# Batch normalisation, one core: loads and stores without pacing waits

## The chip, the cores and the metric

The kernel runs on one core of a Trainium2 chip. The metric is the device time of one execution in microseconds (us), the median of several runs. Lower is better. The chip's profiler also recorded one execution; all views of the profile come from that one.

## The reference

The input is 32 images of 256 channels of 128 x 128 float32 values. Each channel is scaled and shifted by stored statistics:

```
mean, var, gamma, beta: one value per channel (256)
out = gamma * (x - mean) / sqrt(var + 1e-5) + beta      # x, out: (32, 256, 128, 128) float32
```

So every element is read once, multiplied by `scale = gamma / sqrt(var + eps)` of its channel, has `shift = beta - mean * scale` added, and is written once: 537 MB in and 537 MB out.

## The kernel before

A tile is half the channels of one image: 128 channels on the 128 partitions, with the 16384 pixels of each as one row of 64 KB. A tile has 8.4 MB, and there are `NT` = 64 of them (`order` lists them: the first 128 channels of all images, then the others). Three buffers `t0`, `t1`, `t2` (`NBUF` = 3) take them in turn; tile i lies in buffer i mod 3 and is computed in place.

Nothing is scheduled by a tool; each engine works down its own list, and semaphores hold it.

- **SyncE** issues the loads (queue q1 of the profile). Tile 0 comes in two halves (lines 87 and 94) with the four small vectors of statistics between them (line 90), then tiles 1 and 2 (line 96). From tile 3 on there are two waits for each load: on `stored` (line 102), which counts that the store of tile i-3 has left the buffer, and on `vdone` (lines 103 and 104), which counts VectorE's pieces: the load of tile i goes out when VectorE has done the first piece of tile i-1.
- **VectorE** computes `scale` and `shift` once (lines 106 to 124), then the left part of each tile with `tensor_scalar` (line 129). A tile has a first piece of `STEP` = 2560 columns, which waits for the tile's landing, and a second up to column `VCOLS` = 14336. In the last tile the second ends at `VLAST` = 9216. Tile 0 has two pieces of its own, one for each half that lands.
- **ScalarE** computes the rest of each tile with `activation` (line 140), 2048 columns, and 7168 in the last tile. Before the last tile it waits for both of VectorE's pieces (line 161) and for the store of tile i-1 to have landed (lines 163 and 164). Then it issues the store of the whole tile (line 153, queue q10), which waits for `adone`, its own computation. So there is one store at a time. In the last tile ScalarE starts when the tile lands, beside VectorE, and the store waits for both.

So at most one load and one store are under way at a time after the first three loads, and ScalarE, though it computes last, runs only once a store has landed. At the end SyncE waits for the last stores (line 171) and clears the semaphores. One transfer moves 128 rows of 64 KB over 16 DMA engines, 8 rows on each.

Of the kernel before, what the change touches and what calls it, by code (L numbers as in the profile page):

```python
# [8 lines left out]
NBUF = 3  # L9
PAD = 936  # L10


STEP = 2560
VCOLS = 14336
VLAST = 9216

# [2 lines left out]
def kernel(  # L19
# [9 lines left out]
    nc = tc.nc  # L29
# [8 lines left out]
    NT = N * NCB  # L38
# [5 lines left out]
    xr = x.rearrange("n (cb p) h w -> (n cb) p (h w)", p=P)  # L44
    outr = out.rearrange("n (cb p) h w -> (n cb) p (h w)", p=P)

    def tile_of(name, *shape):
        return nc.alloc_sbuf_tensor(name, list(shape), f32)
# [11 lines left out]
    bufs = [tile_of(f"t{s}", P, HW) for s in range(NBUF)]  # L60
# [4 lines left out]
    loaded = [sems[f"loaded{s}"] for s in range(NBUF)]  # L65
    stored = [sems[f"stored{s}"] for s in range(NBUF)]
    early, vdone, adone, fetched, vec, act = (sems[n] for n in names[2 * NBUF :])
# [5 lines left out]
    def step(inst, sem=None, value=None):  # L73
        if sem is not None:
            inst._wait_ge(sem, value)
        elif count[0]:
            inst._wait_ge(vec, count[0])
        inst.then_inc(vec, 1)
        count[0] += 1
        return count[0]  # L80

    left, right = slice(0, HW // 2), slice(HW // 2, HW)
    last = NT - 1
    order = [n * NCB + cb for cb in range(NCB) for n in range(N)]

    with tc.tile_critical():  # L86
        nc.sync.dma_start(out=bufs[0][:, left], in_=xr[order[0]][:, left]).then_inc(early, 16)
        zeroed = step(nc.vector.memset(rows[:], 0.0))  # L88
        for r, ap in enumerate((running_var, gamma, beta, running_mean)):
            inst = nc.sync.dma_start(out=rows[0:NE, r * C : (r + 1) * C], in_=ap.partition_broadcast(NE))  # L90
# [8 lines left out]

    for i in range(NBUF, NT):  # L100
        s, turn = i % NBUF, i // NBUF
        nc.sync.wait_ge(stored[s], 16 * turn)
        inst = nc.sync.dma_start(out=bufs[s][:], in_=xr[order[i]]).then_inc(loaded[s], 16)
        inst._wait_ge(vdone, 2 * (i - 1) + 1)

    step(nc.vector.memset(eps_t[:], eps))  # L106
    step(nc.vector.transpose(out=turned[:], in_=rows[:]), fetched, 16 * NPAR)  # L107
# [3 lines left out]
    for q in range(NQ):  # L111
# [3 lines left out]
        out=std_t[:],  # L115
        in_=var_t,
# [7 lines left out]
    ready = step(nc.vector.tensor_sub(out=shift_t[:], in0=beta_t, in1=ms_t[:]))  # L124
    nc.vector.wait_ge(vec, ready)

    def vector_part(i, first, end):
        t, cb = bufs[i % NBUF], order[i] % NCB
        return nc.vector.tensor_scalar(  # L129
            out=t[:, first:end],  # L130
            in0=t[:, first:end],
            scalar1=scale_t[:, cb : cb + 1],
            scalar2=shift_t[:, cb : cb + 1],
            op0=mybir.AluOpType.mult,
            op1=mybir.AluOpType.add,
        ).then_inc(vdone, 1)

    def scalar_part(i, first):
        t, cb = bufs[i % NBUF], order[i] % NCB
        return nc.scalar.activation(  # L140
            out=t[:, first:],
            in_=t[:, first:],
            func=mybir.ActivationFunctionType.Identity,
            bias=shift_t[:, cb : cb + 1],
            scale=scale_t[:, cb : cb + 1],
        ).then_inc(adone, 1)

    def landed(i):
        return loaded[i % NBUF], 16 * (i // NBUF + 1)

    def store(i):
        s = i % NBUF
        nc.scalar.dma_start(out=outr[order[i]], in_=bufs[s][:])._wait_ge(adone, i + 1).then_inc(stored[s], 16)
# [1 line left out]
    vector_part(0, 0, HW // 2)._wait_ge(early, 16)  # L155
    vector_part(0, HW // 2, VCOLS)._wait_ge(*landed(0))
    for i in range(1, NT):
        vector_part(i, 0, STEP)._wait_ge(*landed(i))
        vector_part(i, STEP, VLAST if i == last else VCOLS)
    for i in range(last):  # L160
        nc.scalar.wait_ge(vdone, 2 * (i + 1))
        inst = scalar_part(i, VCOLS)
        if i:
            inst._wait_ge(stored[(i - 1) % NBUF], 16 * ((i - 1) // NBUF + 1))
        store(i)
    scalar_part(last, VLAST)._wait_ge(*landed(last))
    nc.scalar.wait_ge(vdone, 2 * NT)
    store(last)

    for s in range(NBUF):  # L170
        nc.sync.wait_ge(stored[s], 16 * ((NT - s + NBUF - 1) // NBUF))
# [31 lines left out]
```

## Time and profile before

| | |
|---|---|
| median of 3 runs | 2481.28 us (2480.5 to 2481.8) |
| the profiled execution: its own time | 2480.81 us |
| its span in the profile | 2479.5 us |
| VectorE (DVE) busy | 508.7 us (21%) |
| ScalarE (ACT) busy | 139.8 us (6%) |
| moved by the DMA engines | 1073.85 MB, 433 GB/s over the span |
| a load, issue to landing | 37.0 us (median) |
| a store, issue to landing | 36.5 us (median) |

The span runs from the first to the last instruction that the profiler recorded; the execution's own time has 1.31 us more around it. Busy times count computing instructions only: an engine that waits for a semaphore or issues a transfer is not busy. "Issue to landing" is the time from the issuing instruction until the transfer's semaphore is full, and so has in it the time in which the transfer stands in its queue or shares the DMA engines with another. In the lists of waits and instructions, a name with a q behind it (SPq, ACTq) is the engine's sequencer, which issues transfers.

### The profile page before, as it was taken

What the parts mean: (1) busy time and instruction counts of PE and PEld (TensorE: products, weight loads), DVE (VectorE), ACT (ScalarE), POOL (GpSimd) and SP (SyncE); (2) the same over time, 40 slices, a digit from 0 to 9 for tenths busy, and PEclk for the clock granted to TensorE, in tenths of its full rate; (3) what the DMA queues carried; (4) which work ended last, traced back from release to release, by engine and by line L of the source; (5) the groups of instructions that cost most, each with busy time, mean ns of one, the idle gap of its engine ahead of it and who ended that gap; (6) DMA issues with size and microseconds to landing.
All of it is one profiled execution on the core that took longest, in us unless ns stands there. A gap on an engine that the chain in (4) does not pass through costs nothing.

```text
span 2479.5 us, 514 instructions
## 1 busy us (share of the span) xinstructions
DVE 508.7 (21%) x139; ACT 139.8 (6%) x66; POOL 0.2 (0%) x4
## 2 busy tenths in 40 slices
DVE  2122121221212212122121221212212122121220
ACT  0000000000000000000000000000000000000001
POOL 0000000000000000000000000000000000000000
DMA  9999999999999999999999999999999999999999
GB/s 412 435 438 427 437 438 429 436 438 429 435 438 430 435 439 430 433 438 433 431 438 432 432 438 432 432 438 432 432 438 433 431 438 433 431 438 435 430 438 410
DMA packets 18708, 1073.85 MB, mean 433 GB/s; under 512 B 2128, under 2 KB 2192, under 8 KB 2192
## 3 DMA queue, kind: packets, MB, share of 16 engines
q1 hardware_dynamic: 9488, 536.94, 50.1%
q10 hardware_dynamic: 9216, 536.88, 50.0%
q14 instruction: 4, 0.03, 0.0%
HBM read 536.94 MB, written 536.87 MB: 433 GB/s over the span
## 4 chain that ended last, share of the span: by engine, by line
DMA 92%; DVE 4%; another core or an unknown queue 2%; ACT 0%; issue 0%; SPq 0%; DVEq 0%
DMA t<-in_x_dram 92%; DVE t L129 4%; ACT t L140 0%; SPq L90 0%; DVE rows L88 0%; DVEq L98 0%; SPq L86 0%
## 5 line engine op out<-in xcount | busy, mean ns | idle before, releaser
L129 DVE TENSOR_SCALAR t<-t,scale_t,shift_t 128x11776 f32<-128x11776 f32 (+2 forms) x128 | 505.2, 3989 | 1928.4 <-DMA t<-in_x_dram 1928.3
L140 ACT ACTIVATE t<-t,shift_t,scale_t 128x2048 f32<-128x2048 f32 x64 | 138.2, 2159 | 2297.3 <-DMA out_dram<-t 2274.5
L107 DVE STREAM_TRANSPOSE turned<-rows 32x1024 f32<-32x1024 f32 x1 | 1.2, 1232 | 7.6 <-DMA rows<-in_running_mean_dram 7.6
L114 ACT ACT_TABLE_LOAD x1 | 1.3, 1283 | 6.4 <-PEq L98 6.4
L88 DVE MEMSET rows<- 32x1024 f32 x1 | 0.9, 912 | 1.2 <-SPq L86 1.2
L106 DVE MEMSET eps_t<- 128x1 f32 x1 | 0.1, 59 | 4.4 <-PEq L98 4.4
L114 ACT ACTIVATE std_t<-par,eps_t 128x2 f32<-128x2 f32 x1 | 0.3, 295 | 8.5 <-DVE par L112 8.5
L112 DVE COPY par<-turned 32x8 f32<-32x8 f32 x4 | 0.7, 162 | 0.1
L121 DVE RECIPROCAL rstd_t<-std_t 128x2 f32<-128x2 f32 x1 | 0.2, 165 | 0.4 <-ACT std_t L114 0.4
L122 DVE TENSOR_TENSOR scale_t<-par,rstd_t 128x2 f32<-128x2 f32 x1 | 0.2, 161 | 0.0
L123 DVE TENSOR_TENSOR ms_t<-par,scale_t 128x2 f32<-128x2 f32 x1 | 0.2, 161 | 0.0
L124 DVE TENSOR_TENSOR shift_t<-par,ms_t 128x2 f32<-128x2 f32 x1 | 0.2, 160 | 0.0
L187 POOL MEMSET const-bfloat16-1.0<- 128x1 bf16 x1 | 0.1, 101 | 0.0
L187 POOL MEMSET const-uint8-127<- 128x1 uint8 x1 | 0.1, 101 | 0.0
L187 POOL MEMSET const-float32-0.0<- 128x1 f32 x1 | 0.1, 98 | 0.2 <-issue 0.2
L187 POOL MEMSET const-float32-1.0<- 128x1 f32 x1 | 0.1, 98 | 0.0
## 6 DMA issues: line engine op xcount, KB each, us to landing
t<-in_x_dram SPq DMA_DIRECT2D x2, 4096.0 KB, 16.0
out_dram<-t ACTq DMA_DIRECT2D x64, 36.5
t<-in_x_dram SPq DMA_DIRECT2D x63, 37.0
rows<-in_running_var_dram SPq DMA_DIRECT2D x1, 16.0 KB, 11.2
rows<-in_gamma_dram SPq DMA_DIRECT2D x1, 16.0 KB, 11.0
rows<-in_beta_dram SPq DMA_DIRECT2D x1, 16.0 KB, 10.7
rows<-in_running_mean_dram SPq DMA_DIRECT2D x1, 16.0 KB, 10.7
```

The costliest lines, as they stand in the source:

```text
L88: zeroed = step(nc.vector.memset(rows[:], 0.0))
L106: step(nc.vector.memset(eps_t[:], eps))
L107: step(nc.vector.transpose(out=turned[:], in_=rows[:]), fetched, 16 * NPAR)
L112: placed = step(nc.vector.tensor_copy(out=flat[q * B : (q + 1) * B], in_=blocks[:, :, q, 0]))
L114: nc.scalar.activation(out=std_t[:], in_=var_t, func=mybir.ActivationFunctionType.Sqrt, bias=eps_t[:], scale=1.0,)._wait_ge(vec, placed).t ...
L121: step(nc.vector.reciprocal(out=rstd_t[:], in_=std_t[:]), act, 1)
L122: step(nc.vector.tensor_mul(out=scale_t[:], in0=gamma_t, in1=rstd_t[:]))
L123: step(nc.vector.tensor_mul(out=ms_t[:], in0=mean_t, in1=scale_t[:]))
L124: ready = step(nc.vector.tensor_sub(out=shift_t[:], in0=beta_t, in1=ms_t[:]))
L129: return nc.vector.tensor_scalar(out=t[:, first:end], in0=t[:, first:end], scalar1=scale_t[:, cb : cb + 1], scalar2=shift_t[:, cb : cb + 1 ...
L140: return nc.scalar.activation(out=t[:, first:], in_=t[:, first:], func=mybir.ActivationFunctionType.Identity, bias=shift_t[:, cb : cb + 1] ...
L187: nc = _bacc.Bacc("TRN2", target_bir_lowering=False, num_devices=1)
```

## The change

The waits that hold transfers back for another reason than their data are taken out:

- a load (from tile 3 on) waits only for the store of the tile that was in its buffer before;
- VectorE computes its part of a tile (from tile 1 on) in one piece, so `vdone` counts one for each tile, and two for tile 0;
- ScalarE computes its part of every tile when the tile lands, beside VectorE (once, ahead of them all, it waits until `scale` and `shift` are there, with `vec`); it no longer waits for the store of the tile before;
- a store goes out when both parts of its tile are computed, whatever other stores are under way.

The columns of each engine, the buffers, the order of the tiles and the first loads stay as they are.

```diff
-STEP = 2560
 VCOLS = 14336
 VLAST = 9216
...
     for i in range(NBUF, NT):
         s, turn = i % NBUF, i // NBUF
-        nc.sync.wait_ge(stored[s], 16 * turn)
-        inst = nc.sync.dma_start(out=bufs[s][:], in_=xr[order[i]]).then_inc(loaded[s], 16)
-        inst._wait_ge(vdone, 2 * (i - 1) + 1)
+        nc.sync.dma_start(out=bufs[s][:], in_=xr[order[i]])._wait_ge(stored[s], 16 * turn).then_inc(loaded[s], 16)
...
     vector_part(0, 0, HW // 2)._wait_ge(early, 16)
     vector_part(0, HW // 2, VCOLS)._wait_ge(*landed(0))
     for i in range(1, NT):
-        vector_part(i, 0, STEP)._wait_ge(*landed(i))
-        vector_part(i, STEP, VLAST if i == last else VCOLS)
-    for i in range(last):
-        nc.scalar.wait_ge(vdone, 2 * (i + 1))
-        inst = scalar_part(i, VCOLS)
-        if i:
-            inst._wait_ge(stored[(i - 1) % NBUF], 16 * ((i - 1) // NBUF + 1))
+        vector_part(i, 0, VLAST if i == last else VCOLS)._wait_ge(*landed(i))
+    nc.scalar.wait_ge(vec, ready)
+    for i in range(NT):
+        scalar_part(i, VLAST if i == last else VCOLS)._wait_ge(*landed(i))
+        nc.scalar.wait_ge(vdone, i + 2)
         store(i)
-    scalar_part(last, VLAST)._wait_ge(*landed(last))
-    nc.scalar.wait_ge(vdone, 2 * NT)
-    store(last)
```

## The prediction

> **What bounds the kernel now.** I read the page first.
>
> ```profile
> span 2479.5 us, 514 instructions
> ...
> DMA  9999999999999999999999999999999999999999
> ...
> DMA packets 18708, 1073.85 MB, mean 433 GB/s; under 512 B 2128, under 2 KB 2192, under 8 KB 2192
> ## 3 DMA queue, kind: packets, MB, share of 16 engines
> q1 hardware_dynamic: 9488, 536.94, 50.1%
> q10 hardware_dynamic: 9216, 536.88, 50.0%
> ```
>
> The 16 DMA engines are full in every slice; loads (q1) and stores (q10) take half each, 100.1% together. VectorE works 21% and ScalarE 6% of the span. A large packet is one 64 KB row of a tile, so each engine serves 8 packets of a load and 8 of a store. 100.1% x 2479.5 x 16 over about 16,390 such packets is 2.42 us each; the packet records of the trace have 2.418 us almost throughout, load or store, one queue busy or both.
>
> Then the chain in order of time (start, length, what), for the beat of the middle:
>
> ```profile
> 1017.41 36.98 DMA t<-in_x_dram
> 1056.06 36.97 DMA t<-in_x_dram
> ...
> 2369.72 37.33 DMA t<-in_x_dram
> ```
>
> These are loads 27, 28 and 62, 35 beats from first to last: (2369.72 - 1017.41) / 35 = 38.637 us, or 2.4148 us for each of 16 packets. 1024 packets per engine make 2472.7 us. The span is that, plus 1.95 us to the first packet, 4.4 us that the slowest engine loses, and 0.46 us after the last packet (2479.04). By the records, progress falls behind the beat by 4.1 us in the first 40 us (1.99 of it before the first packet) and by only 0.6 us from there to 2440. So no steady gap exists to be closed.
>
> The waits of SyncE's queue show what the pacing does:
>
> ```profile
> SPq L102 <- DMA out_dram<-t: 1395.0, 61, 66.0
> SPq L103 <- DVE t L129: 984.8, 61, 16.5
> ```
>
> For each of 61 loads it first waits for the buffer's store, then a mean 16.1 us longer (984.8 / 61) for VectorE's 2560-column piece of the previous tile. Last, the timeline at both ends (start, us, engine, line):
>
> ```profile
> 23.45 3.48 DVE L129 TENSOR_SCALAR t<-t,scale_t,shift_t 128x6144 f32<-128x6144 f32 x1 [1.44 <-DMA t<-in_x_dram]
> 26.96 2.09 ACT L140 ACTIVATE t<-t,shift_t,scale_t 128x2048 f32<-128x2048 f32 x1 [10.40 <-DVE t L129]
> 29.09 0.38 ACTq L153 DMA_DIRECT2D out_dram<-t  x1
> ...
> 2407.08 7.93 DVE L129 TENSOR_SCALAR t<-t,scale_t,shift_t 128x2560 f32<-128x2560 f32 x2 [31.06 <-DMA t<-in_x_dram]
> 2431.18 2.09 ACT L140 ACTIVATE t<-t,shift_t,scale_t 128x2048 f32<-128x2048 f32 x1 [36.52 <-DMA out_dram<-t]
> 2433.30 0.34 ACTq L153 DMA_DIRECT2D out_dram<-t  x1
> 2445.70 6.36 ACT L140 ACTIVATE t<-t,shift_t,scale_t 128x7168 f32<-128x7168 f32 x1 [12.43 <-DMA t<-in_x_dram]
> 2445.70 5.27 DVE L129 TENSOR_SCALAR t<-t,scale_t,shift_t 128x2560 f32<-128x2560 f32 x2 [30.69 <-DMA t<-in_x_dram]
> ...
> 2452.09 0.34 ACTq L153 DMA_DIRECT2D out_dram<-t  x1
> ```
>
> Store 62 starts only 12.4 us before load 63 lands (2433.30 against 2445.70), so most of it is still to move then, and the engines have work until store 63 is in its queue.
>
> **The change part by part.** *Waits of the loads.* With the VectorE wait gone, load i goes out when store i-3 has landed, on average 16.1 us earlier, and queues behind load i-1. The engines are full without it, so it buys nothing in the middle. Behind the remaining wait on SyncE stand only later loads.
>
> *Waits of ScalarE and the stores.* ScalarE's 2048 columns (2.09 us) no longer wait for VectorE or for the last store; they run inside VectorE's 7.93 us. A store then goes out about 0.1 us after VectorE: 8.0 us after landing, not the 26.2 us of tile 62 (2433.30 - 2407.08). The store's new waits hold up only ScalarE's next tile, which lands a beat of 38.6 us later. ScalarE's new wait for the factors ends at 17.3 us, before tile 0 lands at 23.45. Merging VectorE's two pieces saves one start in 63 tiles, beside transfers: nothing on the path.
>
> *The order on the engines.* This is the part that decides. Call r the packets of a store that an engine still has when it ends its share of the load under way. The queues alternate packet by packet, so r is set at the start: it is the load packets that ran alone before the store began. Two readings of the records: a transfer can be chosen 1.0 us after its issue (L87 issued at 0.95, first packet 1.95), and an engine chooses its next packet when it starts the present one (store 0, issued at 29.09, was taken by engines that started a packet at 30.17 or later, not by those at 30.13). Now store 0 is issued when VectorE ends, 23.45 + 3.48 + 0.06 = 26.99, and can be chosen from 28.0. Load 1's packets start at 22.3 to 23.1 and each 2.415 us on; the third ones, 27.10 to 27.95, have then chosen another load packet, and the fourth choose the store. Four load packets run alone: r = 4.
>
> Does r hold? After load i's last data the engine runs one store packet and then the small packet that signals landing (2.41 + 0.47 = 2.88 us from the last data of load 63, 2442.82, to the compute at 2445.70). Three store packets are left; alternating with the next load, and with a load packet after them, they give until 6 x 2.415 = 14.5 us to choose the next store. It is there after 0.47 + 7.93 + 0.1 + 1.0 = 9.5 us: 5.0 us of cover. If cover failed, loads would run meanwhile and r would rise; the engines would not idle. Load i+3 is queued when load i+2 still has about four packets, 19 us in alternation, to go. So no idle time between 40 us and the end, and this part costs 0.
>
> *The tail.* After load 63's signal three store packets remain, with no load beside them: 7.24 us. Store 63 needs 0.47 + 6.36 + 0.06 + 1.0 = 7.9 us. The engines wait 0.65 us. In the profile of before six packets remained (2479.04 - 2445.23 is 14 packets, 8 of them of store 63), 14.5 us: the pacing's cover was 6.6 us more than needed. A restart of all idle engines together may cost more: the first packets of load 0 took 1.3 to 2.0 us where later halves took 1.21, and progress lost 0.74 us. I take half, 0.4, between 0 and 0.74.
>
> *The start.* Some eighteen load packets took 2.5 to 3.6 us when store 0 began (30 to 38 us), 0.77 us of progress. Store 0 still begins beside load 1: I take no change, bounds -0.8 and +0.8.
>
> Sum: 0 + 0.65 + 0.4 + 0 = +1.05 us on the profiled 2480.81 (span 2479.5 and 1.31 outside it), or 2481.9; the median of the runs is 0.47 above that execution, so 2482.3. The bounds give 2481.1 to 2483.5.
>
> [...]
>
> **The rivals.** *An engine order one packet shorter.* If store 0 can be chosen before 27.95, the last engine takes it one packet sooner: r = 3. It holds (12.1 us against 9.5), and in the tail two packets, 4.83 us, stand against 7.9: +3.1, with the restart up to +3.8, that is 2484.4 to 2485.1. For it: the margin at the start is 0.05 us on that one engine. Against: 26.99 already takes the hand-overs between engines at their shortest in this trace (0.03 us).
>
> *Slower: packets slow down when both queues are never empty.* Place: load packets while a store runs beside them. Price: the 0.77 us at store 0's beginning, if each of 62 later stores paid it, is 48 us: 2529. It decides from 0.08 us per tile (4.96 us over 62). For it: the one moment of before with two loads queued and a store beginning is where packets took 3.6 us, and load 4 had such packets at 133 to 138 us with none queued. Against: load 2 stayed queued until 54 us and from 39 us on packets took 2.418 us again, and mixed stretches later do too.
>
> *Faster: the gap between loads counts.* A load is under way 36.97 of 38.64 us; closing 1.66 us in 61 tiles would give 101 us, 2380. Against: stores fill those gaps; of the whole span only 4.4 us is neither packets nor the unchanged ends, less than 0.2% (4.96 us), about what a measurement of this kernel can tell from no change. [...]
>
> *The change does nothing:* the order settles with r of 5 or more, the tail is covered: 2480.5 to 2481.5.
>
> **How the numbers follow.** Forecast 0.48; r = 3, 0.20; no effect 0.04; slower packets 0.27; faster 0.01. The first three lie within 0.2%: 0.72. Slower 0.27, faster 0.01. For the range I start at 2480.0 (the start's -0.8 and a little). Of the slower packets I count 0.10 for up to 0.17 us per tile (10.7 us), which ends at 2492; above it 0.17 is left out. The likeliest sign's own range is 2480.0 to 2485.5.
>
> **What would show it.** Right: beat still 38.64 us; loads some 63 us from issue to landing, because they queue; ScalarE beside VectorE; a DMA dip of under 1 us just before store 63 (about 2457 to 2459). The last load lands about 7 us later than before, at 2452.5. r = 3 shows as a dip of 3 us. Wrong: a beat above 38.72, or GB/s below 430 in middle slices (slower packets), or a last store that starts more than 4 us after store 62 ends.

## The result, and the profile after

The change makes the kernel slower: 2504.94 us (median of 3 runs, 2504.41 to 2506.76) against 2481.28, a ratio of 1.0097 with a 95% interval of 1.0074 to 1.012. The forecast was 2482.3 us, with 2492 at the range's upper end. The profiled execution took 2504.94 us, its span is 24.1 us longer than before's 2479.5, and that is the difference to explain.

The page of the changed kernel, with the same parts as were shown of before (span; DMA busy tenths and GB/s in 40 slices; queue, packets, MB, share of 16 engines):

```profile
span 2503.6 us, 392 instructions
...
DMA  9999999999999999999999999999999999999997
GB/s 420 435 432 430 428 433 436 432 435 433 435 433 436 436 433 429 429 435 436 432 432 425 436 435 426 430 435 435 433 423 433 426 430 435 431 428 432 434 430 319
...
q10 hardware_dynamic: 9216, 536.88, 49.8%
q1 hardware_dynamic: 9488, 536.94, 49.7%
```

The engines are full in 39 slices, as before. The last slice (62.6 us) is not: 319 GB/s where the rest has about 432, so (1 - 319/432) x 62.6 = 16 us of all engines' work are missing there, 13 more than before (410 GB/s in its last slice). The other 11 us lie in the middle: seven slices after the first ten have 423 to 429 GB/s, where before has none under 430. The same row of before:

```profile
GB/s 412 435 438 427 437 438 429 436 438 429 435 438 430 435 439 430 433 438 433 431 438 432 432 438 432 432 438 432 432 438 433 431 438 433 431 438 435 430 438 410
```

SyncE's waits (total us, times, longest), and the DMA issues (count, median us from issue to landing):

```profile
SPq L101 <- DMA out_dram<-t: 2385.8, 61, 63.7
```

```profile
out_dram<-t ACTq DMA_DIRECT2D x64, 45.7
t<-in_x_dram SPq DMA_DIRECT2D x63, 63.3
```

The wait for VectorE is gone (984.8 us before), and every load stands in its queue for a tile's time: 63.3 us from issue to landing, as forecast (some 63). This part of the mechanism is as predicted. The timeline's end is not (start, us, engine, line):

```profile
2437.84 2.10 ACT L137 ACTIVATE t<-t,shift_t,scale_t 128x2048 f32<-128x2048 f32 x1 [37.38 <-DMA t<-in_x_dram]
...
2445.68 0.34 ACTq L150 DMA_DIRECT2D out_dram<-t  x1
2476.47 6.36 ACT L137 ACTIVATE t<-t,shift_t,scale_t 128x7168 f32<-128x7168 f32 x1 [36.53 <-DMA t<-in_x_dram]
2476.47 5.08 DVE L126 TENSOR_SCALAR t<-t,scale_t,shift_t 128x9216 f32<-128x9216 f32 x1 [30.88 <-DMA t<-in_x_dram]
2482.86 0.34 ACTq L150 DMA_DIRECT2D out_dram<-t  x1
```

ScalarE and VectorE start together, and store 63 follows them by 0.03 us, both as forecast. But load 63 lands at 2476.5 where 2452.5 was forecast. What the DMA engines did until then shows in windows of 2 us (window, length, busy us of DVE, ACT, POOL, clock, DMA share, GB/s):

```profile
2466.00:2468.00 2.00, 0.00 (x0) 0.00 (x0) 0.00 (x0) 1.00 0.23 98
2468.00:2470.00 2.00, 0.00 (x0) 0.00 (x0) 0.00 (x0) 1.00 0.15 66
2470.00:2472.00 2.00, 0.00 (x0) 0.00 (x0) 0.00 (x0) 1.00 0.15 66
2472.00:2474.00 2.00, 0.00 (x0) 0.00 (x0) 0.00 (x0) 1.00 0.15 66
```

A DMA share of 0.15 is about two engines of 16 (two packets of 64 KB in 2 us are 66 GB/s). Fourteen had nothing left to do from about 2468 on, and waited some 15 us for two that were behind: one sent its last packet of load 63 by 2466.7, the other by 2473.7, and both had packets of store 62 left besides.

The packet records say who they are. Each transfer has a small signal packet on each engine (4 bytes; 1024 of them for the 64 stores), so the landing of one load can be read per engine (first, median and last of the 16, us):

| load | before | after | f3 (below) |
|---|---|---|---|
| 7 | 276.7 / 277.1 / 281.3 | 286.3 / 286.6 / 289.3 | |
| 13 | 508.5 / 509.0 / 513.1 | 513.3 / 513.6 / 528.0 | |
| 19 | 740.3 / 740.8 / 744.9 | 740.3 / 740.7 / 764.5 | |
| 31 | 1204.0 / 1204.5 / 1208.6 | 1202.3 / 1202.4 / 1230.3 | |
| 63 | 2440.4 / 2440.9 / 2445.2 | 2447.7 / 2448.0 / 2476.1 | 2449.7 / 2450.1 / 2454.0 |

Before, the last engine is 4 us behind the median all along. After, two engines fall back, the slower one to 28 us at load 31, and stay there. A load counts as landed when the last engine has signalled: load 63's last signal comes at 2476.1, 28 us after its first, and VectorE and ScalarE, which wait for the full count, start at 2476.47.

Joining each packet to the one that started where it ended gives the 16 engines' own sequences (inferred: the records don't name the engine). Time lost on an engine is then what its stretched packets (64 KB packets of over 2.43 us) took above 2.418 us, and its gaps after its first packet (us):

| | stretched before 1200 us | after 1200 | gaps | sum |
|---|---|---|---|---|
| before, slowest engine | 1.3 | 0.7 | 1.5 | 3.5 |
| after, slowest engine | 16.2 | 9.3 | 1.7 | 27.2 |
| after, second slowest | 12.9 | 8.3 | 5.7 | 26.9 |
| after, mean of the 14 others | 1.5 | 9.6 | 16.1 | 27.2 |

The slowest engine is idle for only 1.7 us in all; it loses 23.7 us more than before's, and the span is 24.1 us longer. Its loss has two parts: about 15 us of its own before 1200 us, and 8 to 10 us that all engines lose after that. The others spend the 15 us idle at the end, waiting for it. (Its 28 us in the landing of loads are twice its 14 us of work behind, because it alternates: beside each load packet that it is behind it also moves a store packet. It signals the end of store 62 at 2483.3, the median engine at 2468.0.) In all 547 packets of 64 KB took over 2.43 us, against 51 before.

### The profile page after: what moved, and what is told of

Read it like the earlier page. It is cut to its first block, busy times and chain, and to the rows that moved or that the text cites. A ratio compares the mean times of both kernels' runs of the same rounds, so it can differ in the third digit from the quotient of the medians.

```text
span 2503.6 us, 392 instructions
## 1 busy us (share of the span) xinstructions
DVE 496.9 (20%) x76; ACT 140.0 (6%) x66; POOL 0.2 (0%) x4
## 4 chain that ended last, share of the span: by engine, by line
another core or an unknown queue 79%; DVE 19%; DMA 1%; ACT 0%; issue 0%; SPq 0%; ACTq 0%; DVEq 0%
DVE t L126 19%; DMA t<-in_x_dram 1%; ACT t L137 0%; SPq L89 0%; DVE rows L87 0%; ACTq L150 0%; DVEq L97 0%; ACTq L159 0%; SPq L85 0%
## 5 line engine op out<-in xcount | busy, mean ns | idle before, releaser
L126 DVE TENSOR_SCALAR t<-t,scale_t,shift_t 128x14336 f32<-128x14336 f32 (+2 forms) x65 | 493.4, 7590 | 1970.9 <-DMA t<-in_x_dram 1970.8
## 6 DMA issues: line engine op xcount, KB each, us to landing
t<-in_x_dram SPq DMA_DIRECT2D x63, 63.3
```

What stands on the lines that cost most here:

```text
L126: return nc.vector.tensor_scalar(out=t[:, first:end], in0=t[:, first:end], scalar1=scale_t[:, cb : cb + 1], scalar2=shift_t[:, cb : cb + 1 ...
```

## The experiments

Theories at the start: the pacing kept the engines in step, and without it some fall behind (the **lag theory**; the expectations call it straggler); against it, that one of the two removed waits matters by itself, that ScalarE or VectorE beside each other slow the DMA engines, that two full queues do, or that only the tail is lost. All ratios are against before on the same chip. Where a run has VectorE in two pieces again (a1, a4, b1, b2, a5), it has them in every tile.

**a1_load_wait**, the change with the load's old wait restored:

```diff
+        nc.sync.wait_ge(stored[s], 16 * turn)
+        inst = nc.sync.dma_start(out=bufs[s][:], in_=xr[order[i]]).then_inc(loaded[s], 16)
+        inst._wait_ge(vdone, 2 * (i - 1) + 1)      # VectorE in two pieces again
```

> The change with one part undone: VectorE in two pieces again and each load waiting for VectorE's first piece of the tile before; ScalarE and the stores stay unpaced. Theory (straggler): in the changed kernel one DMA engine gets longer packets while it is out of step with the others and its lag, 24 us at the end, sets the time; any wait that makes all engines begin a load together once per tile stops the lag from growing, so this gives 2482 to 2487 (a store is then under way for less time after the last landing, which can cost up to 4 us in the tail). Rival (the number of stores queued, not of loads, is what hurts): about 2505. Rival (ScalarE computing beside VectorE disturbs the packets): about 2505.

Measured: 2602.54 us, ratio 1.0481 (1.0466 to 1.0497).

**a2_store_wait**, the change with ScalarE's old waits restored (VectorE's part, the last store):

```diff
+        nc.scalar.wait_ge(vdone, i + 2)
+        inst = scalar_part(i, VCOLS)
+        if i:
+            inst._wait_ge(stored[(i - 1) % NBUF], 16 * ((i - 1) // NBUF + 1))
```

> The change with the other part undone: ScalarE waits for VectorE and for the store of the tile before, as in the kernel before, so that one store is under way at a time; loads stay unpaced, two in the queue. Theory (straggler): all engines begin a store together once per tile, and the lag does not grow: 2479 to 2484. Rival (two loads standing in the queue make packets slow): about 2505.

Measured: 2719.12 us, ratio 1.095 (1.0916 to 1.0983). Either half of the change costs five to ten times as much as the whole. That was in no theory: both were expected at 2479 to 2487, or at 2505 by the rivals. The timeline of this kernel around one landing shows what happens there:

```profile
1517.51 7.75 DVE L126 TENSOR_SCALAR t<-t,scale_t,shift_t 128x14336 f32<-128x14336 f32 x1 [35.41 <-DMA t<-in_x_dram]
1519.93 0.33 SPq L101 DMA_DIRECT2D t<-in_x_dram  x1
1519.94 2.10 ACT L137 ACTIVATE t<-t,shift_t,scale_t 128x2048 f32<-128x2048 f32 x1 [41.08 <-DMA out_dram<-t]
1522.07 0.34 ACTq L150 DMA_DIRECT2D out_dram<-t  x1
```

and its windows there:

```profile
1516.50:1518.00 1.50, 0.49 (x1) 0.00 (x0) 0.00 (x0) 1.00 0.10 44
1518.00:1519.50 1.50, 1.50 (x1) 0.00 (x0) 0.00 (x0) 1.00 0.01 0
1519.50:1521.00 1.50, 1.50 (x1) 1.06 (x1) 0.00 (x0) 1.00 0.80 262
```

A load lands at 1517.5 and the store at 1519.9, with nothing queued behind either: both streams run dry together (DMA share 0.01). Tile after tile this makes 128 us of gaps and 100 us of stretched packets on each engine (means), nearly all of the span's 226 us more; the two load packets after each gap take mostly 3.0 to 3.5 us.

**a3_act_after_dve**, the change with ScalarE after VectorE, but no wait for the last store:

```diff
-        scalar_part(i, VLAST if i == last else VCOLS)._wait_ge(*landed(i))
         nc.scalar.wait_ge(vdone, i + 2)
+        scalar_part(i, VCOLS)
```

> The changed kernel, with ScalarE computing a tile only after VectorE (but not waiting for the last store). No transfer waits for another one. Theory (straggler) and the rival of two queued loads: nothing re-aligns the engines, 2500 to 2508. Rival (ScalarE beside VectorE disturbs the packets): back to 2480 to 2485.

Measured: 2502.68 us (2496.77 to 2511.72), ratio 1.0085 (1.006 to 1.011). The same loss as the change, so ScalarE beside VectorE isn't its cause. Here the spread of load landings stays at 2.7 us until about 1200 us and then grows, on four engines, to 26.7 us at load 63: it doesn't set in at a fixed time.

**a4_paced_last12**, the change with both old waits for tiles from 52 on (`PACED(i)` is `i >= 52`):

```diff
+        if PACED(i):
+            inst._wait_ge(vdone, 2 * (i - 1) + 1)
...
+        if PACED(i):
+            nc.scalar.wait_ge(vdone, 2 * (i + 1))
+            inst = scalar_part(i, VCOLS)
+            inst._wait_ge(stored[(i - 1) % NBUF], 16 * ((i - 1) // NBUF + 1))
```

> Both pacing waits are there for the tiles 52 to 63 and not for those before; ScalarE starts at the landing up to tile 51. Theory (straggler): the lag of the slow engine has grown for 52 tiles and cannot be made up, since that engine never idles: 2498 to 2506. Rival (the loss is only the uncovered end: store 63 starts too late because the last load lands late): pacing before the end restores the cover, 2481 to 2485.

Measured: 2510.88 us, ratio 1.0109 (1.0091 to 1.0126). The engines are in step again at the end (load 63 lands 2475.4 to 2480.3, against 1907.3 to 1935.4 for load 49), but the fast ones now idle their 14 to 16 us earlier, where the pacing begins: some 11 us at 2005 and 4 at 2057. The time is above the expected 2498 to 2506, and far from the rival's 2481 to 2485. So the time is not lost in the tail: most of it is lost on the slow engine, and shows wherever the others next wait for it.

**b1_paced_first24**: the reverse, both old waits for tiles below 24 only (`PACED` is `i < 24`).

> Both pacing waits for the tiles 0 to 23, none for 24 to 63. Theory (an engine that falls out of step with the others gets longer load packets, and unpaced nothing stops its lag from growing): the lag grows in the 40 unpaced tiles only, 2485 to 2505, with all engines landing together until tile 23 and one or two falling behind after it. Rival (the lag comes from the start, where all engines move in step; pacing over the start cures it): 2479 to 2483.

Measured: 2491.21 us (2482.99 to 2499.95, 7 runs), ratio 1.0048 (1.0026 to 1.007). In the profiled execution (2487.5) one engine lost some 7 us in a burst of stretched packets at 900 to 1000 us, where the pacing ends, and none after: from load 31 on the landings stay 2.2 us apart without any pacing. So the lag can grow in unpaced tiles but needn't. The time is as expected (2485 to 2505).

**c1_no_compute**, the change without VectorE's and ScalarE's work on the tiles; the store waits for the load alone:

```diff
     for i in range(NT):
+        nc.scalar.dma_start(out=outr[order[i]], in_=bufs[s][:])._wait_ge(*landed(i)).then_inc(stored[s], 16)
```

> The changed kernel's loads and stores without the computation on the tiles: a store waits for its tile's landing alone, and the output is a copy of the input. Theory (lag from the transfers themselves): one or two engines still fall behind by 10 us or more, 2485 to 2505. Rival (VectorE and ScalarE working in SBUF make packets long): all packets take 2.42 us, 2476 to 2480.

Measured: 2504.73 us, ratio 1.0091 (1.007 to 1.0111). The whole loss with no computation: neither engine's work matters. Here too the last load's signals lie 30 us apart (2450.2 to 2480.2).

**c2_loads_alone**, the loads with no stores but the last three (a load waits for the load before it in its buffer), and **c3_stores_alone**, the stores with only the first three loads, nothing computed in either:

```diff
-..._wait_ge(stored[s], 16 * turn).then_inc(loaded[s], 16)
+..._wait_ge(loaded[s], 16 * turn).then_inc(loaded[s], 16)        # c2
+            inst._wait_ge(stored[s], 16 * (i // NBUF))           # c3
```

> 64 loads, each waiting only for the load before it in its buffer, no computation, and stores of the last three tiles alone. 67 transfers of 8 packets of 2.4148 us are 1294 us, with the ends about 1300. Theory (a load packet is stretched by other engines' stores beginning): no engine falls behind, spread of a landing over the engines under 3 us, 1298 to 1302. Rival (one engine is slower by nature): its landings fall behind by some 10 us over the 64 loads and the time is 1305 to 1315.

> Three loads and then 64 stores from the three buffers, each waiting only for the store before it in its buffer, no computation. 67 transfers are 1294 us of packets, about 1300 with the ends. Theory (a packet is stretched only where loads and stores meet): every store packet takes 2.42 us and the engines land within 3 us of each other, 1297 to 1303. Rival (stores have a slow engine): over 1305.

Measured: 1301.29 us (2 runs) and 1300.63 (1 run). The landings of one transfer lie at most 0.8 us apart throughout, and c2 has five stretched packets ahead of its stores. One direction alone doesn't fall out of step, so a slow engine as such is ruled out.

**d1_unlinked**, 64 loads into two buffers and 64 stores from the third, two of each always queued, nothing computed, and no wait between loads and stores:

```diff
+        ...in_=xr[order[i]])._wait_ge(loaded[s], 16 * turn)...   # s alternates 0, 1
+        inst = nc.scalar.dma_start(out=outr[order[i]], in_=bufs[2][:])
+        if i >= 2:
+            inst._wait_ge(stored[s], 16 * (i // 2))
```

> 64 loads into two buffers and 64 stores from a third, no computation, and no wait between loads and stores: both queues always hold two transfers. Same bytes as the kernel. Theory (lag from the mix of the two directions alone): engines fall behind as in the changed kernel, 2485 to 2515. Rival (the lag needs the loop in which a load waits for a store and a store for a load): all engines stay together, 2475 to 2480.

Measured: 2483.14 us (8 runs), ratio 1.0003 (0.9993 to 1.0013); load spread 3.4 us, constant from 500 us on. This lies between the two expected ranges, but the engines stay together. Two full queues as such cost next to nothing, against the slower rival's wording.

**e3_order_plain**, the change with the tiles in plain order:

```diff
-    order = [n * NCB + cb for cb in range(NCB) for n in range(N)]
+    order = list(range(NT))
```

> The changed kernel with the tiles in plain order (both halves of the channels of one image one after the other), so that the addresses of a load and of the store beside it stand 8 MB nearer together. Theory (the long packets come from the order in which the engines turn from loads to stores, not from the addresses): an engine falls behind as before, 2498 to 2510. Rival (the long packets are collisions of addresses in memory): the number of long packets changes much, and the time goes under 2490 or over 2520.

Measured: 2512.58 us, ratio 1.0129 (1.0111 to 1.0147); load 63 lands between 2456.3 and 2485.5. That is a little above the expected 2498 to 2510, and inside the rival's limits: not the addresses of the tiles, as far as this order tells.

**a5_both_waits_act_early**, before with ScalarE computing at the landing; its wait for the last store moved from the computation to the store:

```diff
+        scalar_part(i, VLAST if i == last else VCOLS)._wait_ge(*landed(i))
+        nc.scalar.wait_ge(vdone, 2 * (i + 1))
+        if 0 < i < last:
+            nc.scalar.wait_ge(stored[(i - 1) % NBUF], 16 * ((i - 1) // NBUF + 1))
```

> Both pacing waits back, but ScalarE computes a tile at its landing, beside VectorE, as in the change; the wait for the store of the tile before stands ahead of the store alone. A store then goes out about 2.1 us sooner after the last one than in the kernel before. Theory (the pair of waits is what keeps the two queues apart in phase and the engines together; ScalarE's place is nothing): the beat is 38.64 us and the time 2479 to 2484. Rival (ScalarE's late start is part of the pacing): 2490 or more.

Measured: 2603.08 us, ratio 1.0493 (1.0475 to 1.0512). A miss. Both waits are back, each stream has a common start, and it is as slow as a1. So waits that keep the engines in step are not enough.

**b2_paced_every8**, both old waits in every eighth tile (`PACED` is `i % 8 == 7`).

> Both pacing waits for every eighth tile only (7, 15, ... 63), none for the others. Theory (the lag of an engine grows slowly when unpaced, and a paced tile makes the engines begin together again): the lag cannot be taken back but has less time to grow, 2484 to 2500. Rival (each passage between the two manners costs a burst of long packets, as in the kernel paced for 24 tiles, which had one): eight passages of 1 to 2 us, 2490 to 2515. Rival (pacing of some tiles keeps nothing): 2500 to 2508 as in the changed kernel.

Measured: 2537.47 us, ratio 1.0222 (1.0206 to 1.0238), worse than no pacing at all and above every range that was expected. Most engines idle about 25 us in the middle and 16 at the end. Why each return to the pacing costs so much isn't known.

**The balance theory.** a1, a2 and a5 have something in common that before and the change lack. Call a stream's *pause* the time from an engine's signal packet of one transfer to the moment at which it can choose the next one of that queue. Its parts are 0.47 us from the signal to what waits for it (load 63 of before; 0.37 to 0.49 over its loads 1 to 63), whatever the issue waits for besides, 0.05 or 0.1 us of hand-overs, and 1.0 us from the issue (tile 0 of before: issued at 0.95, first packet at 1.95; store 63 of after took 0.85). In before a load's pause is 0.47 + 1.52 (VectorE's first piece, 7.93 for both less 6.41 for the second) + 0.1 + 1.0 = 3.1 us, and a store's 0.47 + 2.09 (ScalarE) + 0.05 + 1.0 = 3.6: both between one packet and two. By the records an engine's packets follow each other end to end, 2.415 us apart, and while an engine is busy a transfer's first one starts where another ends (store 0 of before, issued at 29.09, at 32.74 to 35.79 on the 16 engines). So, by the theory, both pauses cost the other stream the same number of packets, and the two keep their distance; where the pauses fall on different sides of a multiple of 2.415, one stream gains on the other from tile to tile until both run dry together. The landing of store i-1 minus that of load i, per tile, shows it (us):

| | first tiles | then constant at | load pause, store pause |
|---|---|---|---|
| before | 16.7, 24.3, 25.0 | 24.1 | 3.1, 3.6 |
| after | 14.5, 14.9, 14.5 | 14.5 to 16 | none, none |
| a1 | 14.5, 9.7, 2.4, 10.1, 2.4 | 4.8 | 3.1, none |
| a2 | 14.6, 24.4, 34.7, 42.1 | 44.5 | none, 3.6 |
| a5 | 14.5, 15.0, 9.7 | 4.8 | 3.1, 1.5 |

The slow three sit at one of two ends. To test this, VectorE's first piece alone was made shorter (**f1_step512**, `STEP = 512`, its row 0.55 us: load pause 2.1, store's 3.6) or longer (**f2_step8192**, `STEP = 8192`, 4.55 us: 6.1 against 3.6) in the kernel before, with no wait added or taken away; and then balance was given back at the longer pause (**f4_step8192_vcols11776**, ScalarE's part made 4608 columns, 4.23 us: 6.1 against 5.8).

```diff
-STEP = 2560
+STEP = 512           # f1; 8192 in f2 and f4
-VCOLS = 14336
+VCOLS = 11776        # f4 alone
```

> The kernel before with STEP = 512: a load's pause after the last landing is shorter by 1.1 us, all waits stay. Theory (balance): an engine switches queues at packet ends, 2.41 us apart, and has chosen one packet ahead; a load can be chosen 0.47 + 0.33 + 0.19 + 1.0 = 2.0 us after the landing (under one packet), a store 0.47 + 2.09 + 0.04 + 1.0 = 3.6 us (over one). So the load queue rests one packet less than the store queue, loads run ahead by a pair of packets (4.8 us) per tile until both queues run dry together, and the time goes towards the 2719 us of the kernel that paced stores only: 2600 to 2720. Rival (it is the waits as such that keep the engines together): 2479 to 2484.

> The kernel before with STEP = 8192: the load's pause is longer by 3.1 us. Theory (balance): a load can be chosen 0.47 + 4.55 + 0.19 + 1.0 = 6.2 us after the landing (over two packets), a store after 3.6 us (over one): stores run ahead by 4.8 us per tile until both queues run dry together, as in the two kernels at 2603: 2560 to 2640. Rival (the waits as such): 2479 to 2486.

> The kernel before with STEP = 8192 and VCOLS = 11776, so that ScalarE has 4608 columns (about 4.3 us) after VectorE: both pauses are longer. A load can be chosen 6.2 us after the landing, a store about 0.47 + 4.3 + 0.04 + 1.0 = 5.8 us: both over two packets. Theory (balance): the pauses are equal in packets again and the time is back at 2479 to 2486, in spite of both pauses being longer than in any slow kernel. Rival (a long pause of the loads is what hurts): as with STEP = 8192 alone, over 2550.

Measured: f1 2694.49 us (ratio 1.0852, 1.0834 to 1.087), f2 2679.37 (1.0794, 1.0778 to 1.081; more than was expected), f4 2484.41 (1.0006, 0.9996 to 1.0015). One number makes the kernel before 8% slower, and a second one that lengthens the other pause gives it back. The distances went as they should: f1 to 39.8 us, f2 to 4.9, f4 constant at 26.6. In f1 the middle engine's distance grows by 4.8 us a tile at first (19.3, 24.1, 29.1), a pair of packets, as the theory has it. That the multiples of 2.415 us decide, and not the size of the difference, isn't shown: the pauses differ by 0 to 0.5 us in the balanced kernels (before, f3, f4) and by 1.5 us or more in the others, and no run has a small difference across a multiple. SyncE's waits of f1:

```profile
SPq L102 <- DMA out_dram<-t: 2380.3, 61, 65.9
SPq L103 <- DVE t L129: 203.5, 61, 15.3
```

of f2:

```profile
SPq L103 <- DVE t L129: 2467.5, 61, 42.0
SPq L102 <- DMA out_dram<-t: 112.7, 29, 65.8
```

and of f4:

```profile
SPq L102 <- DMA out_dram<-t: 1362.9, 61, 66.5
SPq L103 <- DVE t L129: 1021.4, 61, 17.3
```

In f1 nearly all of a load's wait ends with the store, in f2 with VectorE, and f4 shares it out as before did (1395.0 and 984.8). So this view tells where the two streams of a kernel stand.

**f3_direct_waits**, the lag theory's own test: the changed kernel, but each load waits also for the load before it, and each store for the store before it, so that each transfer has a common start and both pauses are the same shortest ones (0.47 + 0.05 + 1.0 = 1.5 us):

```diff
         nc.sync.wait_ge(stored[s], 16 * turn)
+        nc.sync.wait_ge(loaded[(i - 1) % NBUF], 16 * ((i - 1) // NBUF + 1))
...
+        if 0 < i < last:
+            nc.scalar.wait_ge(stored[(i - 1) % NBUF], 16 * ((i - 1) // NBUF + 1))
         store(i)
```

> Both queues paced with the shortest pause: a load waits for the load before it, a store for the store before it, each on the transfer's own semaphore; ScalarE computes beside VectorE, VectorE in one piece. Both can be chosen 1.5 us after the landing. Theory (balance): equal pauses, so the order of the queues stays as it was set at the start (a store lands about 15 us after the load beside it) and all engines begin each transfer together: no engine falls behind, 2480 to 2487 (the cover at the end may be short by up to 4 us). Rival (the long pauses are needed): over 2500.

Measured: 2484.62 us (10 runs), ratio 1.0011 (1.0002 to 1.0021), as expected. Some 20 of the 24 us come back. Its timeline at the end:

```profile
2454.42 6.36 ACT L139 ACTIVATE t<-t,shift_t,scale_t 128x7168 f32<-128x7168 f32 x1 [36.52 <-DMA t<-in_x_dram]
...
2460.81 0.34 ACTq L152 DMA_DIRECT2D out_dram<-t  x1
```

and its windows from there on:

```profile
2450.00:2455.00 5.00, 0.58 (x1) 0.58 (x1) 0.00 (x0) 1.00 1.00 433
2455.00:2460.00 5.00, 4.50 (x1) 5.00 (x1) 0.00 (x0) 1.00 1.00 433
2460.00:2465.00 5.00, 0.00 (x0) 0.78 (x1) 0.00 (x0) 1.00 1.00 433
```

Load 63 lands at 2454.4 instead of 2476.5, and no engine runs out of work before store 63. Stretched packets come to at most 6.3 us on an engine, instead of 25.5.

What the runs establish: the loss needs loads and stores (c2, c3), linked by their buffers (c1 has the links and d1 hasn't; but d1's stores also trail its loads by 84 us, where c1's trail by 5 to 8); it needs no computation (c1) and not this order of tiles (e3); it is lost on a few engines first, and the others wait for those (after, a3, a4); a wait of each transfer for the one before it, with equal pauses, prevents most of it (f3); with unequal pauses it does far more harm than it saves (a1, a2, a5, f1, f2). One rival is left, that the distance keeps the engines in step and not the common start: the kernels whose spread grows have their stores 5 to 17 us behind the loads, before and f3 settle at 24.1 and 16.9, and b1's unpaced tiles keep their step at 32.0. Against it: a3 stood at 17.2 for 1200 us and then lost its step, and a4's paced last tiles stand at 14.5 with a constant spread of 4.8 us, though they are only a few. No run separates the two. None of the versions that move the same bytes is faster than the kernel before.

## Why the prediction was wrong, and where it was right

- **What bounds the kernel**: right. The DMA engines do, in both kernels (100.1% and 99.5% of the 16 engines' span), and nothing was gained in the middle. The faster rival (2380) is out: loads issued earlier stood longer in their queue (63.3 us from issue to landing, 37.0 before), and the kernel became 1% slower.
- **Waits of the loads**, costed at 0 because the engines are full without them: the premise is right and the conclusion wrong. That a wait buys no bandwidth does not make it useless: it started each transfer on 16 engines together, with a load's signals within 5 us of each other where after has up to 28 (or, by the rival that is left, it set the distance of the two streams). The same holds for **waits of ScalarE and the stores**, where the two pauses had also to match; that the change takes out both is why it costs 24 us and not the 120 to 240 of either alone (a1, a2).
- **The order on the engines**, r = 4: right while the engines were in step. Store i-1 lands 14.5 us after load i from the first tiles on, where the working had 3 store packets and as many load packets, 14.5 us; on the slowest engine this still holds for load 62. The rivals r = 3 and r of 5 or more are out.
- **The step that failed** stands ahead of the sum: "4.4 us that the slowest engine loses", taken over from before as a constant, because progress fell behind by only 0.6 us after the first 40 us. In the sum itself it is the 0 of "this part costs 0". By the table of losses, the slowest engine lost 3.5 us before and 27.2 after. With the 23.7 us more, the forecast is 2506, against 2504.9.
- **The tail**: the mechanism held, with another engine to wait for. Forecast: three packets of store 62, 7.24 us, after load 63's signal, and 7.9 us until store 63's first packet. Measured on the slowest engine: the signal at 2476.10, the end of store 62 at 2483.34 (7.24 us), store 63's first packet on any engine at 2483.71 (7.6 us). **The restart**, for which 0.4 was taken, cost 0.03 us: the first packets of store 63 took 2.445 to 2.455 us, nearly all later ones 2.418. So the wait on the slowest engine was about 0.4 us instead of 0.65; but 14 engines were idle for about 15 us.
- **The start**, 0: right. The stretched packets there cost 0.72 us instead of 0.77, and up to 210 us the middle engine's beat is 38.64 us (the slowest engine's is 39.0 already).
- **The slower rival** had the right kind and place (stretched packets while both queues are full, from 0.08 us per tile) and 0.27 of the chance. Measured, the slowest engine lost 23.7 us over 62 tiles, 0.38 per tile. It was priced as a cost of all engines at every store's start (48 us); it was that of two engines up to 1200 us, then a smaller one of all. Against it, the prediction held that mixed stretches later ran at 2.418 us: those stretches were paced ones. Of its 0.27, 0.17 was left out above the range, where the result fell.
- **The signs** named for being wrong: two of three came true, middle slices below 430 GB/s and a beat above 38.72 us (39.05 between the landings of loads 1 and 63). The third, a store 63 more than 4 us after the end of store 62, didn't on the slowest engine (0.4 us), though 14 engines had ended store 62 some 15 us before. The forecast and its range were missed.

**Open**: what stretches a packet. In after, about a third of the first store packets of a tile took over 2.43 us on the fast engines (none before), and 8.6% of the first load packets on all engines. On the slowest engine it is the loads: 44 of its 63 first packets of a load and 30 of the fifth ones were stretched, which makes 20 of its 25.5 us. These are places in the order, not causes. Other engines beginning a store don't account for it: up to 600 us only 7 of 43 stretched load packets lay beside 12 or more such beginnings. Open too is why one engine is the first to fall behind, why d1's two queues keep in step without any common start, and what b2 pays at each return to the pacing.

## What to carry to other kernels

Here the DMA engines were full (100.1% of the span of 16), and taking waits out gained no bandwidth (433 GB/s before, 429 after). It lost what the waits did besides: they started each transfer on all 16 engines together (a load's signals within 5 us of each other, up to 28 without), and kept loads and stores at a fixed distance (24.1 us). Before touching such a wait, read the landing of a transfer per engine (in after, 28 us of spread at load 63 went with some 15 us in which 14 engines were idle) and the two waits of the load queue (which of them ends last), and change the pauses of loads and stores only together (a load's of 6.1 us took 2679 us beside a store's of 3.6, and 2484 beside 5.8). A retuned tile split is such a change too: `STEP` from 2560 to 8192 columns, with the same waits, cost 8%.

## What the hardware showed that was not expected

- DMA engines of one core need not keep in step by themselves: with the same 1016 packets of 64 KB, they ended load 63 up to 28 us apart (after), against 5 us with pacing.
- An engine alternates between two queues one 64 KB row of 2.418 us at a time (in before, all 4573 times that a row of one transfer ended with rows left of a load and a store already begun, the next row was the other's, by the joined records). A load pause that is 1 us shorter (f1) cost a whole pair of packets (4.8 us) per tile at first, and in the end both streams ran dry together: load pauses of 2.1, 3.1 and 6.1 us beside a store's 3.6 gave 2694, 2481 and 2679 us.
- After all engines had run dry together (a2), the next two load packets took mostly 3.0 to 3.5 us instead of 2.42, so each such gap costs nearly as much again in stretched packets: 128 us and 100 us per engine. The restart with store 63 in the changed kernel, a store with no load beside it, cost only 0.03 us.
